# Rows scaled before they are turned, pair 1's keys ahead of a gate and its values ahead of pair 2's keys, and one inversion for head pairs 0 and 1

## The chip, the cores and the metric

The kernel runs on one core of a Trainium2 chip. A core has five engines with instruction streams of their own: TensorE (PE; its weight loads are listed as PEld), VectorE (DVE), ScalarE (ACT), GpSimd (POOL) and SyncE (SP), which issues nearly all the transfers here. The metric is the device time of one execution in microseconds; less is better.

## What is computed

One step of a decoder trunk of two layers, for a prompt of 1024 tokens and a sample group of 8 x 4 tokens, model width 1024, all in float32. Layer 0 is sliding-window attention, layer 1 a gated DeltaNet. Both have the form

```python
h = rms_norm(x, g) * (1 + scale[:, None]) + shift[:, None]   # shift, scale, gate = silu(c) @ w_mod + b_mod
x = x + gate * ((branch(h @ w_in) * silu(z)) @ w_out)
```

The DeltaNet has 8 key heads and 16 value heads of width 128 (two value heads to a key head), a causal convolution of four taps on q, k and v, and runs over chunks of tokens:

```python
lower = where(strict, (kb @ k.T) * decay, 0)                 # kb = k * beta
sol = triangular_solve(lower + I, rhs, lower=True, unit_diagonal=True)
u = w_v - w_k @ S                                            # w_v, w_k are the columns of sol
o = q_dec @ S + (q @ k.T * decay) @ u
S = S * g_tot + k_dec.T @ u
```

The last three lines are a chain: each chunk needs the state S of the one before.

## The kernel before, in words

**Projections.** The 1056 tokens are held transposed (model width on the partitions), in three groups of 384, 384 and 288. A projection takes 128 columns of a weight matrix; the float32 product is made of three products of split halves (high x high, high x low, low x high), so 128 columns cost 8 x 3 x 3 = 72 matmuls into the PSUM tiles `ps_pj`. ScalarE splits off the weights' high half (`wh`), GpSimd forms the low half (`wl`).

**Start (lines 600 to 740).** SyncE loads the nine tiles of x, `xt`, 128 tokens of 1024 each and 32 of the sample, then the modulation weights `wm` in two halves, the second into the buffers of the x rows as these come free. `scale_x` (627) takes the rows' norm `rs` and builds a diagonal `dg = ident * rs` of 128x128; `turn_x` (642) multiplies xt by it in float32, which scales and transposes at once: eight 128x128 blocks a tile, four to a PSUM bank, a "half tile" below. VectorE or ScalarE copies the result to `zo`. Then come the modulation steps (L344), their end (350 to 375), `shape_h` (662), which makes the split `hhi`, `hlo`, and the first projections (L702).

**The planner.** From the first attention projection on every instruction is issued through the class `Core` (96), which is why the profile gives all of them line 89. It keeps an estimated clock for each engine and for each tile. Work beside the projections is written as generators, "jobs", that yield a condition; `weave` (485) puts a job in a list by its rank (the tables `K` and `KR`), and after the projection matmuls `stages` lets each job whose condition holds issue its next piece. `ready` and `soon` are conditions on the planned TensorE clock, `idle` on another engine's, `later(n)` is a count of projection steps, and `until` lets jobs run, without projections, till a condition holds. So the order of each engine's instructions is fixed when the kernel is built, and it follows from the conditions, the ranks and the order in which the projections are called.

**End of layer 0.** The output projection takes its PSUM tiles by turns (1448), `add_out` (1336) adds the gated result to the rows, `shape` (1375) norms a tile with a diagonal as above, two packs of four blocks each, and makes `h2hi`, `h2lo`, the input of layer 1, tile by tile in the order 0, 8, 1, 2, 3, then the rest.

**Layer 1.** The 16 value heads go as eight pairs, r = 0 to 7, each with one key head. The loop at 2155 orders the projections; with q, k for the pair's query and key, z, z' for its gates and v, v' for its values it is: k0, q0, z0, z1, k1, v0, v0', q1, z2, z3, k2, v1, v1', q2 and so on, where a z pair is named by its place among the gates. `plan` (1631) is the same order for the weights' loads. Two lines hold a projection back:

```python
if what == "k":
    until(lambda: finished[0] >= r - 1)
```

so the keys of pair r + 1 wait until the chain of pair r - 1 is through. Beside these run, for each pair:
- the taps of the convolution (`vT<-XR,cT,vT` on VectorE),
- `solve` (1832), which builds the triangular blocks of 128 tokens for 8 blocks and 2 heads in `UZ`, and sends the sixty-four 32x32 diagonal blocks to DRAM,
- `invert` (1882), which loads these as `X`, one block to a partition (64 partitions), clears the blocks in UZ by 16 memsets on GpSimd, and inverts them by forward substitution on VectorE: 31 steps of two instructions (`tmp<-X`, then `X<-X,tmp`). The result goes to DRAM (`Xdd`) and comes back as `Xc`; `diagonal` makes `Xd` of it and multiplies it with UZ (`ps_lg<-Xd,UZ`), `blocks` forms the rest of the inverse (`ps_lg<-UZ,M`),
- `chain` (1984), the walk over the eight chunks with the state S. One chunk is `ps_mi<-S,kT`, `ps_ob<-vo,UZ`, `ps_mi<-us,ktok`, `ps_mi<-S,qT`, `ps_mi<-uo,DP` on TensorE with VectorE's `vo`, `us`, `uo` between.

`finished` counts chains, `inverted` and `solved` the pairs that are through these stages.

Of the kernel before, what the change touches and what calls it, by code (L numbers as in the profile page):

```python
# [219 lines left out]
def body(tc, I, O, cst_ap, dbg=None):  # L220
# [26 lines left out]
    VK = ()  # L247
# [379 lines left out]
    def scale_x(ts):  # L627

        n = len(ts)
        sv = sm.tile([P, 4], F32, tag="sv4", name="sv4")[:, 0:n]  # L630
        nc.vector.tensor_scalar(sv, xss[:, ts[0]:ts[0] + n], 1.0 / D, EPS, ALU.mult, ALU.add)
        rs = sm.tile([P, 4], F32, tag="rs4", name="rs4")[:, 0:n]
        rsqrt(nc, sm, rs, sv, n, tag=f"rx{n}")
        dgs = []
        for q, t in enumerate(ts):
            parts = P if t < NB else TS
            dg = xp.tile([P, P], F32, tag="dg", name="dg", bufs=6)[0:parts, 0:parts]
            last = nc.vector.tensor_scalar_mul(dg, ident[0:parts, 0:parts], rs[0:parts, q:q + 1])
            dgs.append(dg)
        return dgs, last  # L640

    def turn_x(ts, dgs, after):

        for q, t in enumerate(ts):
            parts = P if t < NB else TS
            for kk in range(2):
                pt = psb(("pj3", "lg", "pj3", "lg", "pj3", "ob")[(2 * t + kk) % 6])
                for j in range(4):
                    k = kk * 4 + j
                    mm = nc.tensor.matmul(pt[:, j * parts:(j + 1) * parts], xts[t][:, k * P:(k + 1) * P], dgs[q],  # L650
                                          start=True, stop=True)
# [56 lines left out]
    for i, ts in enumerate(xb):  # L708
        dgs, last = nxt
        if i < 3:  # L710
            nxt = scale_x(xb[i + 1])
        mm = turn_x(ts, dgs, nxt[1])
# [598 lines left out]
    if True:  # L1311
# [24 lines left out]
        def add_out(pj, i, t, hf):  # L1336
# [3 lines left out]
            yield lambda: gathered[0] == 2 * i + hf and i in rows_ and shaped[0] >= i - 1 + hf  # L1340
# [34 lines left out]
        def shape(i, t, xt, ss, parts):  # L1375

            nonlocal x2_guard
# [6 lines left out]
            dg = x2.tile([P, 512], F32, tag="y", name="dg", bufs=2)[0:parts, 0:parts]  # L1384
            nc.vector.tensor_scalar_mul(dg, ident[0:parts, 0:parts], rs)
            for kk in range(2):
                yield ready(dg, xt)
                pt = yield from bank("lg")
                for q in range(4):
                    nc.tensor.matmul(pt[:, q * parts:(q + 1) * parts], xt[:, (4 * kk + q) * P:(4 * kk + q + 1) * P], dg,  # L1390
                                     start=True, stop=True)
# [44 lines left out]
        for i, t in enumerate(turned_):  # L1436
# [7 lines left out]
            for kk, hf in order if i < NB else sorted(order, key=lambda o: o[::-1]):  # L1444
                if True:
                    ns = slice(hf * 512, (hf + 1) * 512)
                    if hf not in pjs:
                        tag = ("pj", "pj", "mi", "mi")[outs[0] % 4]
# [52 lines left out]
    def decays():  # L1501
# [21 lines left out]
        nc.scalar.activation(al, al, AF.Exp)  # L1523
        for gi, (a, b) in enumerate(GRP):
# [109 lines left out]
    for r in range(HQ):  # L1634
        pz, pv = [4096 + 2 * r * P, 4096 + (2 * r + 1) * P], [2 * HQ * P + 2 * r * P, 2 * HQ * P + (2 * r + 1) * P]
        pk = [(HQ + r + 1) * P]
        plan += [r * P] + (pz + (pv + pk if r in VK else pk + pv) if r + 1 < HQ else pv + pz)
# [5 lines left out]
    if True:  # L1643
# [188 lines left out]
        def solve(hq, st):  # L1832
# [47 lines left out]
            weave(invert(hq, st, Ld, Xdd), "invert", hq)  # L1880

        def invert(hq, st, Ld, Xdd):
            UZ, lg = st["UZ"], spare(hq)
            yield lambda: inverted[0] == hq


            X = gs.tile([64, 32, 32], F32, tag="X", name="X")
            tmp = gs.tile([64, 256], F32, tag="tmp", name="tmp")
            nc.sync.dma_start(X, Ld)
            yield soon(X)  # L1890
            nc.gpsimd.memset(X.rearrange("p i c -> p (i c)")[:, 0:1024:33], 1.0)
            for cp_ in range(4):
                uv = UZ[cp_].rearrange("p h c i -> p (h c) i")
                for b in range(4):
                    bs = slice(32 * b, 32 * b + 32)
                    nc.gpsimd.memset(uv[bs, :, bs], 0.0)
            yield soon(X)
            for k in range(31):
# [3 lines left out]
                nc.vector.tensor_tensor(tv, X[:, k, k + 1:].unsqueeze(2).to_broadcast([64, n, m]),  # L1902
                                        X[:, k, 0:m].unsqueeze(1).to_broadcast([64, n, m]), ALU.mult)
                nc.vector.tensor_tensor(X[:, k + 1:, 0:m], X[:, k + 1:, 0:m], tv, ALU.subtract)
            nc.sync.dma_start(Xdd, X)
            inverted[0] += 1
# [7 lines left out]
            def diagonal():  # L1914

                for cp_, uz in enumerate(uzs):
# [12 lines left out]
                    yield soon(pm)  # L1929
                    M = gs.tile([P, 4, 96], F32, tag="M", name="M", bufs=3)  # L1930
# [226 lines left out]
        for r in range(HQ):  # L2157
# [5 lines left out]
            if r + 1 < HQ:  # L2163
                proj_z(2 * r)
                proj_z(2 * r + 1)
# [3 lines left out]
                for what in "vk" if r in VK else "kv":  # L2169
                    if what == "k":  # L2170
# [546 lines left out]
```

## Time and profile before

| | us |
|---|---|
| median of three runs (1730.36 to 1739.1) | 1732.38 |
| the profiled execution's own time | 1730.22 |
| its span | 1728.1 |
| TensorE busy in it | 1628.6 |
| VectorE busy | 1207.9 |
| ScalarE busy | 862.0 |
| GpSimd busy | 603.2 |

The mean granted clock of TensorE is 0.983 of full speed. In a row of a timeline stand the start and the duration in us, the engine, the line, the operation and `out<-in` by the program's names, the shape, `x` and the count of matmuls that follow each other directly, and in brackets the idle time before with what ended it. A float32 matmul of the old `dg` kind has two records. Group rows end with the busy sum and the mean in ns of one, then the idle time just before them. Matmuls are pipelined, so the distance from one start to the next tells more of their cost than the duration.

### The profile page before, as it was taken

What the parts mean: (1) busy time and instruction counts of PE and PEld (TensorE: products, weight loads), DVE (VectorE), ACT (ScalarE), POOL (GpSimd) and SP (SyncE); (2) the same over time, 40 slices, a digit from 0 to 9 for tenths busy, and PEclk for the clock granted to TensorE, in tenths of its full rate; (3) what the DMA queues carried; (4) which work ended last, traced back from release to release, by engine and by line L of the source; (5) the groups of instructions that cost most, each with busy time, mean ns of one, the idle gap of its engine ahead of it and who ended that gap; (6) DMA issues with size and microseconds to landing.
All of it is one profiled execution on the core that took longest, in us unless ns stands there. A gap on an engine that the chain in (4) does not pass through costs nothing. (4 is left out here: it accounts for less than half of the span.)

```text
span 1728.1 us, 31800 instructions
## 1 busy us (share of the span) xinstructions
PE 1628.6 (94%) x10666; PEld 1432.1 (83%) x10666; DVE 1207.9 (70%) x3538; ACT 862.0 (50%) x2514; POOL 603.2 (35%) x1170
## 2 busy tenths in 40 slices
PE   6999999998999899799999999999999998989897
PEld 5988888986777889689989999899998996667685
DVE  4526675564565678877887789778798876357677
ACT  4625555444334565256554665654756555332332
POOL 2601111112122334354443544545345454332322
PEclk9999999999999999899999999999999999999999
DMA  9542121233233232132412323224232137764785
GB/s 330 152 134 72 52 58 50 55 98 106 85 130 103 81 79 67 53 88 56 126 36 75 102 59 107 69 77 112 50 107 62 46 97 211 228 200 130 233 277 184
DMA packets 281573, 191.77 MB, mean 111 GB/s; under 512 B 98362, under 2 KB 253882, under 8 KB 281379
## 3 DMA queue, kind: packets, MB, share of 16 engines
q1 hardware_dynamic: 281410, 189.75, 38.1%
q8 instruction: 84, 1.38, 0.3%
q14 instruction: 79, 0.64, 0.1%
HBM read 144.68 MB, written 47.04 MB: 111 GB/s over the span
## 5 line engine op out<-in xcount | busy, mean ns | idle before, releaser
L89 PE MATMUL ps_pj<-h2hi,wl 128*128 128x384 f32 (+1 forms) x1128 | 380.4, 337 | 2.2 <-POOL wl L89 2.2
L89 PE MATMUL ps_pj<-h2hi,wh 128*128 128x384 f32 (+1 forms) x1128 | 378.3, 335 | 2.1 <-ACT wh L89 2.1
L89 PE MATMUL ps_pj<-h2lo,wh 128*128 128x384 f32 (+1 forms) x1128 | 379.4, 336 | 0.0
L89 POOL TENSOR_TENSOR wl<-wr,wh 128x512 fp32r<-128x512 f32 x122 | 164.4, 1348 | 517.5 <-ACT wh L89 432.9
L89 PEld LDWEIGHTS ps_pj<-h2hi,wl 128*128 128x128 f32 x1128 | 213.6, 189 | 6.2 <-POOL wl L89 3.1
L89 PEld LDWEIGHTS ps_pj<-h2hi,wh 128*128 128x128 f32 x1128 | 213.5, 189 | 4.3 <-ACT wh L89 2.4
L89 PEld LDWEIGHTS ps_pj<-h2lo,wh 128*128 128x128 f32 x1128 | 213.5, 189 | 3.2
L89 POOL TENSOR_TENSOR xt<-xt,y 128x512 f32<-128x512 f32 (+1 forms) x48 | 63.9, 1333 | 188.2 <-DVE y L89 165.1
L89 PE MATMUL ps_pj<-hlo,wh 128*128 128x384 f32 (+1 forms) x360 | 119.0, 331 | 0.0
L89 PE MATMUL ps_pj<-hhi,wh 128*128 128x384 f32 (+1 forms) x360 | 118.4, 329 | 0.0
L89 PE MATMUL ps_pj<-hhi,wl 128*128 128x384 f32 (+1 forms) x360 | 117.9, 328 | 0.0
L89 DVE SCALAR_TENSOR_TENSOR vT<-XR,cT,vT 128x384 f32<-128x384 f32 (+1 forms) x144 | 93.0, 658 | 29.0 <-ACT vT L89 27.1
L89 DVE TENSOR_TENSOR tmp<-X 64x31 f32<-64x31 f32 (+15 forms) x248 | 94.0, 379 | 10.4 <-POOL X L89 7.1
L89 DVE TENSOR_TENSOR X<-X,tmp 64x31 f32<-64x31 f32 (+15 forms) x248 | 94.6, 381 | 8.5
L89 ACT CAST wh<-wr 128x512 fp32r<-128x512 f32 x122 | 75.1, 616 | 16.4 <-PE ps_pj L89 12.0
L89 PEld LDWEIGHTS ps_pj<-hlo,wh 128*128 128x128 f32 x360 | 67.7, 188 | 11.2 <-issue 11.1
L89 ACT COPY XR<-ps_pj 128x384 f32<-128x384 f32 (+1 forms) x96 | 43.0, 448 | 55.9 <-PE ps_pj L89 55.7
L89 POOL TENSOR_TENSOR Xd<-Xc,cst 32x128 f32<-32x128 f32 x128 | 63.4, 495 | 21.2 <-DMA Xc<-Xdd 10.4
L89 PEld LDWEIGHTS ps_pj<-hhi,wh 128*128 128x128 f32 x360 | 67.7, 188 | 2.7 <-issue 2.7
L89 ACT ACTIVATE prob<-prob,nm 128x256 f32<-128x256 f32 (+1 forms) x128 | 62.2, 489 | 14.8 <-DVE nm L89 14.6
L89 PEld LDWEIGHTS ps_pj<-hhi,wl 128*128 128x128 f32 x360 | 67.7, 188 | 2.1 <-issue 2.1
L89 ACT ACTIVATE vo<-vo,fo 128x128 f32<-128x128 f32 x128 | 42.3, 392 | 54.0 <-POOL fo L89 54.0
(574 smaller groups left out, 4218.1 us busy)
## 6 DMA issues: line engine op xcount, KB each, us to landing
wr<-in_gdn_w_in SPq DMA_DIRECT2D x96, 256.0 KB
S<-in_state_gdn_s SPq DMA_DIRECT2D x40, 256.0 KB
xt<-in_x_prompt SPq DMA_DIRECT2D x16, 512.0 KB
wm<-in_w_mod SPq DMA_DIRECT2D x16, 512.0 KB
wr<-in_swa_w_in SPq DMA_DIRECT2D x64, 128.0 KB
wmod<-in_w_mod SPq DMA_DIRECT2D x32, 256.0 KB
wm<-in_w_mod SPq DMA_DIRECT2D x32, 256.0 KB
DP<-gcr SPq DMA_DIRECT2D x64, 128.0 KB
```

The source lines that it names most:

```text
L89: inst = fn(*args, **kwargs)
```

## The change

Five parts, cut to their core:

```diff
-    VK = ()
+    VK = (1,)
...
 def scale_x(ts):
-            dg = xp.tile([P, P], F32, tag="dg", name="dg", bufs=6)[0:parts, 0:parts]
-            last = nc.vector.tensor_scalar_mul(dg, ident[0:parts, 0:parts], rs[0:parts, q:q + 1])
+            if t in (5, 7, 8):
+                nc.scalar.activation(xts[t], xts[t], AF.Copy, scale=rs[0:parts, q:q + 1])
+            else:
+                last = nc.vector.tensor_scalar_mul(xts[t], xts[t], rs[0:parts, q:q + 1])
...
 def turn_x(ts, after):
-                    mm = nc.tensor.matmul(pt[:, j * parts:(j + 1) * parts], xts[t][:, k * P:(k + 1) * P], dgs[q],
-                                          start=True, stop=True)
+                    mm = nc.tensor.transpose(pt[:, j * parts:(j + 1) * parts], xts[t][:, k * P:(k + 1) * P],
+                                             ident[0:parts, 0:parts])
...
 def add_out(pj, i, t, hf):
-            yield lambda: gathered[0] == 2 * i + hf and i in rows_ and shaped[0] >= i - 1 + hf
+            yield lambda: gathered[0] == 2 * i + hf and i in rows_
...
 def shape(i, t, xt, ss, parts):
+                if i < 5:
+                    xn = x2.tile([P, 512], F32, tag="xn", name="xn", bufs=2)[0:parts]
+                    yield idle("vector", rs, xt)
+                    nc.vector.tensor_scalar_mul(xn, xt[:, kk * 512:(kk + 1) * 512], rs)
...
+                    if i < 5:
+                        nc.tensor.transpose(pt[:, q * parts:(q + 1) * parts], xn[:, q * P:(q + 1) * P],
+                                            ident[0:parts, 0:parts])
...
-                        tag = ("pj", "pj", "mi", "mi")[outs[0] % 4]
+                        tag = ("mi", "mi", "pj", "pj")[outs[0] % 4]
...
 def decays():
+        yield later(KD)
         for gi, (a, b) in enumerate(GRP):
...
-        plan += [r * P] + (pz + (pv + pk if r in VK else pk + pv) if r + 1 < HQ else pv + pz)
+        plan += [r * P] + (pz[0:1] + pk + pz[1:] + pv if r == 0 else
+                           pz + (pv + pk if r in VK else pk + pv) if r + 1 < HQ else pv + pz)
...
-            weave(invert(hq, st, Ld, Xdd), "invert", hq)
+            blocks_of.append((hq, st, Ld, Xdd))
+            if hq != 0:
+                weave(invert(list(blocks_of)), "invert", hq)
+                blocks_of.clear()
...
 def invert(systems):
+            first, N = systems[0][0], 64 * len(systems)
+            X = gs.tile([P, 32, 32], F32, tag="X", name="X")[0:N]
+            for i, (_, _, Ld, _) in enumerate(systems):
+                nc.sync.dma_start(X[64 * i:64 * i + 64], Ld)
-            for cp_ in range(4):
-                uv = UZ[cp_].rearrange("p h c i -> p (h c) i")
-                for b in range(4):
-                    bs = slice(32 * b, 32 * b + 32)
-                    nc.gpsimd.memset(uv[bs, :, bs], 0.0)
...
+            for hq, st, _, Xdd in systems:
+                weave(rebuild(hq, st, Xdd), "invert", hq)
...
-                proj_z(2 * r + 1)
+                if r > 0:
+                    proj_z(2 * r + 1)
                 for what in "vk" if r in VK else "kv":
+                    if r == 0 and what == "v":
+                        proj_z(1)
```

- **Start.** The rows are scaled in place, six tiles on VectorE and three (5, 7, 8) on ScalarE, and then turned by transposes against the identity.
- **Shaping.** The first five tiles of `shape` are scaled half a row at a time into `xn` and turned the same way; the other four keep the diagonal. `add_out` no longer waits for `shaped`, and the output projection starts its turns with the other PSUM pair. `decays` starts eight projection steps later.
- **Order.** The projections run k0, q0, z0, k1, z1, v0, v0', q1, z2, z3, v1, v1', k2, q2: k1 and z1 change places, and the values of pair 1 go ahead of k2, whose condition is unchanged.
- **Joint inversion.** Pair 0's blocks wait until pair 1's are built; both are inverted together on 128 partitions. The other pairs are inverted alone, on 64. What came after the inversion in `invert` is now `rebuild`.
- **Memsets.** The 16 clearings of UZ in each pair are gone.

In TensorE's stream at the end of layer 0's output projection, where the projections of layer 1 begin (k0, its weights `kw0h` and `kw0l`), a pack with the diagonal `dg` stood behind the first three of them:

```order
L89 MATMUL ps_pj<-whi,olo 128x512
L89 MATMUL ps_pj<-wlo,ohi 128x512
L89 MATMUL ps_pj<-h2hi,kw0h 128x384
L89 MATMUL ps_pj<-h2lo,kw0h 128x384
L89 MATMUL ps_pj<-h2hi,kw0l 128x384
L89 MATMUL ps_lg<-dg,xt 128x128 x4
L89 MATMUL ps_pj<-h2hi,kw0h 128x384
```

Now that pack stands ahead of them, and the last one comes later, among the steps of the second half (`kw1h`, `kw1l`):

```order
L89 MATMUL ps_pj<-h2hi,kw0l 128x384
L89 MATMUL ps_pj<-h2hi,kw1h 128x384
L89 MATMUL ps_pj<-h2lo,kw1h 128x384
L89 MATMUL ps_pj<-h2hi,kw1l 128x384
L89 MATMUL ps_lg<-dg,xt 128x128 x4
L89 MATMUL ps_pj<-h2hi,kw1h 128x384
```

Between the first projection matmul and this pack there are 39 of them.

In TensorE's stream in the middle of chain 0, two chunks before read:

```order
L89 MATMUL ps_ob<-vo,UZ 128x128 x2
L89 MATMUL ps_mi<-us,ktok 128x256
L89 MATMUL ps_mi<-S,qT 128x256
L89 MATMUL ps_mi<-uo,DP 128x128 x2
L89 MATMUL ps_mi<-S,kT 128x256
L89 MATMUL ps_ob<-vo,UZ 128x128 x2
L89 MATMUL ps_tr<-cst,vo 128x128 x4
L89 MATMUL ps_mi<-us,ktok 128x256
L89 MATMUL ps_mi<-S,qT 128x256
L89 MATMUL ps_mi<-uo,DP 128x128 x2
```

Now one of its chunks is spread among the projection of v1:

```order
L89 MATMUL ps_pj<-h2lo,wh 128x384
L89 MATMUL ps_tr<-cst,vT 128x128 x2
L89 MATMUL ps_mi<-us,ktok 128x256
L89 MATMUL ps_lg<-Xd_6482,UZ 128x96 x4
L89 MATMUL ps_pj<-h2hi,wl 128x384
L89 MATMUL ps_mi<-S,qT 128x256
L89 MATMUL ps_mi<-uo,DP 128x128 x2
L89 MATMUL ps_pj<-h2hi,wh 128x384
L89 MATMUL ps_mi<-S,kT 128x256
L89 MATMUL ps_pj<-h2lo,wh 128x384
```

Five of the eight chunks stand like this; the last three still follow one another without a projection. In VectorE's stream the 62 instructions on X read `128x31` and so on for the two pairs where they read `64x31`, and stand behind the taps of v0':

```order
L89 SCALAR_TENSOR_TENSOR vT<-XR_6021,cT,vT 128x384 x6
L89 TENSOR_TENSOR tmp<-X 128x31
L89 TENSOR_TENSOR X<-X,tmp 128x31
L89 TENSOR_TENSOR tmp<-X 128x60
L89 TENSOR_TENSOR X<-X,tmp 128x30x2
```

45 lines of the change are left out of this document (24 added, 21 removed).

## The prediction

> **What bounds the kernel now.** I read the page first, for which engine is full; then the busy time by stage, for where that engine stands or works at something else; then the timeline of those places. The page (engines as busy us, share, instructions; then TensorE's granted clock in 40 slices):
>
> ```profile
> span 1728.1 us, 31800 instructions
> PE 1628.6 (94%) x10666; PEld 1432.1 (83%) x10666; DVE 1207.9 (70%) x3538; ACT 862.0 (50%) x2514; POOL 603.2 (35%) x1170
> PEclk9999999999999999899999999999999999999999
> ```
>
> TensorE is busy 94% of the span, so a gain has to come from the 99.5 us it stands, or from work that it needn't do or does with pauses that still count as busy. The second kind shows only by stage (stretch, its length, then busy us and count of PE, PEld, DVE, ACT, POOL, the granted clock, the DMA share and GB/s):
>
> ```profile
> 16.00:19.30 3.30, 3.30 (x16) 3.30 (x17) 2.08 (x11) 1.71 (x5) 0.00 (x0) 0.53 1.05 364
> 23.20:34.20 11.00, 10.96 (x96) 10.86 (x96) 7.27 (x24) 3.68 (x8) 0.00 (x0) 1.00 1.07 346
> 440.00:536.00 96.00, 96.00 (x480) 75.56 (x479) 56.67 (x176) 35.91 (x83) 20.71 (x16) 1.00 0.35 113
> 536.00:658.00 122.00, 109.16 (x691) 103.27 (x690) 82.67 (x231) 69.68 (x183) 40.43 (x72) 0.99 0.29 78
> 703.30:754.10 50.80, 38.21 (x280) 29.30 (x281) 41.80 (x126) 17.50 (x63) 15.71 (x54) 0.90 0.20 57
> 754.10:814.00 59.90, 59.55 (x417) 57.00 (x416) 45.93 (x115) 39.56 (x115) 25.76 (x61) 1.00 0.27 69
> ```
>
> Where projections are woven with the rest, TensorE is full: 59.55 of 59.90 us from 754. In 703 to 754 it shows 38.21 of 50.80, and the same stretch for the projections' bank alone shows none of them:
>
> ```profile
> 703.30:754.10 50.80, 0.00 (x0) 0.02 (x1) 0.00 (x0) 0.41 (x1) 0.90 0.20 57
> ```
>
> Its timeline has the last projection matmul, the walk of chain 0 with pauses, and the first of the next projection (start, us, engine, line, operation, in brackets the idle time before):
>
> ```profile
> 702.99 0.29 PE L89 MATMUL ps_pj<-h2hi,wl 128*128 128x288 f32 x1
> ...
> 733.13 0.75 PE L89 MATMUL ps_ob<-vo,UZ 128*128 128x128 f32 x4 [0.44 <-DVE vo L89]
> 734.59 0.70 PE L89 MATMUL ps_mi<-us,ktok 128*128 128x256 f32 x2 [0.70 <-DVE us L89]
> ...
> 737.40 0.74 PE L89 MATMUL ps_ob<-vo,UZ 128*128 128x128 f32 x4 [0.44 <-DVE vo L89]
> ...
> 754.11 0.42 PE L89 MATMUL ps_pj<-h2hi,wh 128*128 128x384 f32 x1
> ```
>
> This is the gate `finished[0] >= r - 1` of k2: after ten projections nothing but chain 0 and the blocks of pair 1 is left to TensorE. One chunk takes 4.27 us there (733.13 to 737.40), each step waiting for VectorE's result.
>
> **The start.** Today 12 half tiles are turned by f32 matmuls in 23.2 to 34.2, 0.89 us each by these rows; transposes of four 128x128 tiles take 0.36 (820.98 to 821.34):
>
> ```profile
> 28.67 1.06 PE L650 MATMUL ps_pj<-dg,xt 128*128 128x128 f32 x8
> 29.56 1.06 PE L650 MATMUL ps_lg<-dg,xt 128*128 128x128 f32 x8
> ...
> 34.23 3.64 PE L344 MATMUL ps_mi<-wm,cT 128*32 128x512 f32 x32
> ...
> 820.98 0.60 PE L89 MATMUL ps_lg<-cst,qT 128*128 128x128 f32 x4
> 821.34 0.42 PE L89 MATMUL ps_pj<-h2hi,wl 128*128 128x384 f32 x1
> ```
>
> On TensorE alone that is 12 x 0.53 = 6.4 us. The scaled rows add work elsewhere; the nearest rows are VectorE's whole-row scale, the diagonal it replaces, and ScalarE's pass over a row:
>
> ```profile
> L671 DVE TENSOR_SCALAR fu<-zo,Sc,Sh 128x1024 f32<-128x1024 f32 x2 | 1.6, 802 | 0.0
> L638 DVE TENSOR_SCALAR dg<-cst,rs 128x128 f32<-128x128 f32 x8 | 1.9, 283 | 0.1
> L625 ACT ACTIVATE sq<-xt 128x1024 f32<-128x1024 f32 x8 | 8.4, 1055 | 1.1 <-DMA xt<-in_x_prompt 1.0
> ```
>
> VectorE gets about three rows more in that stretch, less five diagonals: 7.27 + 2.4 - 1.4 = 8.3 us; ScalarE two rows more, 3.68 + 2.1 = 5.8. So VectorE's evacuations are late next, and the stretch shrinks from 11.0 to no less than about 8.3: -2.7. Beyond that, the modulation steps (3.64 us at 34.23) now stand partly among the transposes, in TensorE's new pauses: up to -3.6 more. And SyncE's queue, with the second half's weights on it, waits for exactly these matmuls to let the rows' buffers go:
>
> ```profile
> SPq L287 <- PE ps_lg L650: 10.1, 5, 4.7
> ```
>
> That is released sooner, but the DMA share is 1.07 already, so it can't bring much. I take -5, from -2 to -7.
>
> The granted clock was 0.53 in the first 3.3 us and 1.00 in the dense stretch; 0.90 where TensorE stood for a quarter (703 to 754). The Trainium skill, "TensorE: Matmul & The Clock Gate", Part 4 on PE-mode transpose, says that a transpose doesn't count as busy for the gate that raises the clock. No row here shows transposes alone, so nothing agrees or disagrees yet; by that rule the start is the second rival below.
>
> **The shaping.** Tiles 0, 8, 1, 2, 3 are turned the same way. The old packs and the only wait in front of one:
>
> ```profile
> L89 PE MATMUL ps_lg<-dg,xt 128*128 128x128 f32 x120 | 16.2, 278 | 2.0 <-DVE dg L89 2.0
> L89 PE MATMUL ps_lg<-dg,xt 32*128 32x32 f32 x16 | 2.1, 274 | 0.0
> 538.97 1.16 PE L89 MATMUL ps_lg<-dg,xt 128*128 128x128 f32 x8 [1.71 <-DVE dg L89]
> 539.88 0.42 PE L89 MATMUL ps_pj<-h2hi,kw0h 128*128 128x384 f32 x1
> ```
>
> A pack costs 0.91 (538.97 to 539.88), so eight save 8 x 0.55 = 4.4, and the sample tile's 2.1 falls to about 0.7. They lie in 440 to 536, where PE is busy 96.00 of 96.00: -5.8 at most. Ten half-row scales on VectorE (about 0.4 each, half of the 802) less five diagonals add 2.6 us to its 56.67 of 96; they are hidden unless a pack waits for its scale as the one above waited 1.71. I take -4.5, from 0 to -5.8. The dropped condition of `add_out` and the swapped banks of the output projection let the last rows be added earlier; the order now has 39 projection matmuls ahead of the last pack instead of three, so the 1.71 goes: -1.5, from 0 to -2. `decays` waiting for `later(KD)` moves small matmuls behind projections: 0.
>
> **The order of pairs 0 and 1.** Keys of pair 1 come before its gate, and v1, v1' before k2. Counted in completed projections, the changed order has chain 0's chunks behind 10.6, 10.9, 11.2, 11.4, 11.6 and then three times 12.0: five lie among v1's and v1' projections, three are bare. Bare: 3 x 4.27 = 12.8 us. The five cost TensorE only their work. Woven packs succeed one another like this:
>
> ```profile
> 823.62 0.59 PE L89 MATMUL ps_mi<-S,kT 128*128 128x256 f32 x2
> 824.05 0.59 PE L89 MATMUL ps_mi<-S,qT 128*128 128x256 f32 x2
> 824.48 0.61 PE L89 MATMUL ps_mi<-uo,DP 128*128 128x128 f32 x4
> 824.84 0.42 PE L89 MATMUL ps_pj<-h2lo,wh 128*128 128x384 f32 x1
> ```
>
> From start to start that is 0.43, 0.43, 0.36. With three packs on the state, two of four small ones and a transposed one (0.36 above) a chunk is 3 x 0.43 + 3 x 0.36 = 2.4 us, five are 12; the blocks of pair 1, an estimated eight packs of about a microsecond, bring it to 20. So the 50.8 become 12.8 + 20 = 33, a gain of 18, if the inversion is in time.
>
> **The joint inversion.** 62 instructions run once on 128 partitions instead of twice on 64, after the taps of v0'. That is the seventh projection, which ends at 658 in the old clock (the row from 536 above covers these seven); with an estimated 7 us for its taps the inversion starts at 665. The old ones (page, mean ns after the busy sum; then single instructions, last the first block that needs the result):
>
> ```profile
> L89 DVE TENSOR_TENSOR tmp<-X 64x31 f32<-64x31 f32 (+15 forms) x248 | 94.0, 379 | 10.4 <-POOL X L89 7.1
> L89 DVE TENSOR_TENSOR X<-X,tmp 64x31 f32<-64x31 f32 (+15 forms) x248 | 94.6, 381 | 8.5
> 630.91 1.30 DVE L89 TENSOR_TENSOR X<-X,tmp 64x112 f32<-64x112 f32 x1
> 681.32 0.27 DVE L89 TENSOR_TENSOR X<-X,tmp 64x112 f32<-64x112 f32 x1
> 682.90 0.18 DVE L89 TENSOR_TENSOR X<-X,tmp 64x31 f32<-64x31 f32 x1
> ...
> 691.91 1.03 PE L89 MATMUL ps_lg<-Xd,UZ 128*128 128x96 f32 x8
> ```
>
> 62 x 0.38 = 23.6 us, about 31 with other work of VectorE between; from the last one to the first block 691.91 - 683.08 = 8.8. Ready: 665 + 31 + 8.8 = 705. TensorE comes to that block when ten projections are done, 703 in the old clock. No row has 128 partitions: if the partitions cost nothing the wait is 0 to 3 us, at the mean of 0.5 it is 10. I take 4, from 0 to 14. Saved on VectorE: 23.6 us, off the path; so is GpSimd's, 128 memsets of 25.2 us:
>
> ```profile
> L89 POOL MEMSET UZ<- 32x128 f32 x128 | 25.2, 197 | 5.4
> ```
>
> This part: -18 + 4 = -14, from -4 to -20. From 14 projections on the two orders run together; the last chain starts 0.17 of a projection later, at 15 us each (754 to 814 is four of them), less what slack takes: +1, from -2 to +3.
>
> **The sum.** -5 - 4.5 - 1.5 - 14 + 1 = -24, from 1730.2 (the profiled execution's own time) to 1706.2. The median shown, 1732.4, is 2.2 above that execution: 1708.
>
> **Rivals.** First: chain 0 isn't covered. If the joint result comes 14 us or more after TensorE asks, or the chunks stall on VectorE as now, the bare stretch only moves: this part gives 0 to -4, the total is -10 to -14, 1718 to 1722. For: VectorE shows 41.80 of 50.80 busy there already, and chain 0 can't begin before both pairs are inverted. Against: 23.6 us less work on it. Chance 0.18.
>
> Second: the start at a low clock. If pauses between transposes keep the clock at the 0.53 of the first row, 12 x 0.36 us double (+4) and the modulation steps too (+3.6, part hidden by VectorE): that part gives -1 instead of -5, 1712. Chance 0.10.
>
> Third, slower: the joint instructions pay for their width, or for GpSimd beside them as the 1.30 against 0.27 above shows, at all 62. At 1.2 us each the result is ready at 665 + 74 + 8.8 = 748, and TensorE waits 45 us at the first block, with v1, v1' and k2 behind it: 45 instead of 4 makes +17, 1749. It turns slower past the bound when the wait exceeds 37 us, at 1.07 us an instruction. Against: one such row of 1.30 in a mean of 0.38. Chance 0.05. The Trainium skill, "SBUF — State Buffer", calls the port pair that VectorE and GpSimd share an exclusive lock, held for a whole instruction; the 1.30 and 0.27 agree.
>
> **The numbers.** Forecast 0.60; the three rivals 0.18, 0.10, 0.05; 0.07 for the small terms all at their poor ends (-2, 0, 0, with -13 and +1: 1718). A measurement tells 0.5% from no change, 8.7 us, so faster is below 1723.7: the forecast, the second rival and most of the first, 0.87; same 0.08; slower 0.05. The best ends together give -7 - 5.8 - 2 - 20 - 2 = -37, 1696; all poor ends without the third rival -3, 1729. Eight in ten: 1698 to 1723.
>
> **What would show it.** In the changed profile: projection matmuls between the chunks of chain 0 and about 13 us without any; the joint instructions near 0.38 us each and no idle above 5 us before the first block; half tiles turned in about 8 us from 23 and the first dense projection near 37; no wait on dg near 539. The forecast is wrong if the first block waits over 14 us, if chunks of chain 0 among projections still take 4 us of TensorE, or if the start ends where it did.

## The result and the profile after

| | before | after |
|---|---|---|
| median, us | 1734.36 (4 runs, 1730.36 to 1739.1) | 1712.32 (4 runs, 1711.98 to 1713.67) |
| the profiled execution | 1730.22 | 1712.31 |
| its span | 1728.1 | 1710.3 |

The ratio is 0.987, 95% interval 0.9845 to 0.9895: faster by 1.3%, clear of the noise, with 22 us between the medians and 17.9 between the profiled executions. A second measurement of the changed kernel gave 1712.54 and 0.9862 (0.9842 to 0.9882). The forecast was 1708, from 1698 to 1723. The profiled execution of the kernel before lies at the low end of its runs (1729.99 to 1741.15 over all of this record), so traces account for 17.9 us; where the rest lies, no trace shows.

The page of the changed kernel:

```profile
span 1710.3 us, 31377 instructions
PE 1613.3 (94%) x10554; PEld 1414.2 (83%) x10554; DVE 1189.9 (70%) x3478; ACT 864.7 (51%) x2517; POOL 578.4 (34%) x1041
```

TensorE's share is what it was. Its busy time fell by 15.3 us and its idle time by 2.5 (99.5 to 97.0): most of what went had counted as busy. The busy time by stage of the changed kernel comes next. The first row goes from the first projection of layer 1 (536.0 in the kernel before) to the end of seven (657.8 before); the others go from ten projections to the last projection matmul of the twelfth, from there to the first of the thirteenth (the stretch that is bare of projections), and on to the end of fourteen:

```profile
531.80:646.50 114.70, 107.74 (x685) 102.70 (x684) 75.80 (x212) 67.99 (x179) 32.19 (x55) 0.99 0.33 83
686.90:740.70 53.80, 53.41 (x486) 47.96 (x485) 35.88 (x88) 25.51 (x75) 25.82 (x57) 1.00 0.21 53
740.70:755.00 14.30, 10.45 (x54) 7.85 (x53) 7.88 (x25) 8.72 (x34) 8.52 (x32) 0.92 0.27 73
755.00:791.80 36.80, 36.14 (x231) 34.44 (x231) 28.09 (x82) 26.85 (x85) 13.47 (x36) 0.99 0.24 72
```

The stretch without projections shrank from 51 us to 14.3. The timeline of the changed kernel has the last projection matmul, the three chunks left over, and the next projection:

```profile
740.72 0.30 PE L89 MATMUL ps_pj<-h2hi,wl 128*128 128x288 f32 x1
740.85 0.61 PE L89 MATMUL ps_ob<-vo,UZ 128*128 128x128 f32 x4
...
745.75 0.61 PE L89 MATMUL ps_ob<-vo,UZ 128*128 128x128 f32 x4
...
751.08 0.75 PE L89 MATMUL ps_ob<-vo,UZ 128*128 128x128 f32 x4 [1.32 <-DVE vo L89]
...
755.04 0.67 PE L89 MATMUL ps_pj<-h2hi,wh 128*128 128x384 f32 x1
```

Counted by completed projections (one is done when the next begins), where both orders have done the same ones, the changed kernel is ahead by 3.4 us at its first dense projection (38.95 against 42.37), 4.2 at the first projection of layer 1, 11.4 after seven, 22.5 after fourteen, 24.3 at the last one, and 17.8 at the end. So 6.4 us are given back behind the last projection. The second measurement has a profile too. It is ahead by 4.6, 7.3, 14.5, 25.6, 26.1 and 17.7 at these places: a lead may differ by 3 us between two executions of one kernel.

### The profile page after: what moved, and what is told of

The parts are those of the page before. It is cut to its first block, busy times and chain, and to the rows that moved or that the text cites. A ratio compares the mean times of both kernels' runs of the same rounds, so it can differ in the third digit from the quotient of the medians.

```text
span 1710.3 us, 31377 instructions
## 1 busy us (share of the span) xinstructions
PE 1613.3 (94%) x10554; PEld 1414.2 (83%) x10554; DVE 1189.9 (70%) x3478; ACT 864.7 (51%) x2517; POOL 578.4 (34%) x1041
## 4 chain that ended last, share of the span: by engine, by line
PE 31%; DVE 8%; DMA 4%; ACT 3%; issue 2%; POOL 2%; SPq 1%; POOLq 0%; ACTq 0%; DVEq 0%
PE ps_pj L89 19%; PE ps_lg L89 4%; PE ps_mi L89 4%; PE ps_tr L89 3%; PE ps_ob L89 2%; DMA S<-in_state_gdn_s 1%; DMA of<-gTd 1%; DMA out_new_s_s<-S 1%; SPq L89 1%; DVE vT L89 1%; DVE tmp L89 1%; DVE UZ L89 1%; POOL rst L89 1%; DVE X L89 1%; ACT L89 0%
## 5 line engine op out<-in xcount | busy, mean ns | idle before, releaser
L89 DVE TENSOR_TENSOR tmp<-X 64x60 f32<-64x60 f32 (+23 forms) x217 | 82.3, 379 | 8.8 <-POOL X L89 5.4
L89 DVE TENSOR_TENSOR X<-X,tmp 64x60 f32<-64x60 f32 (+23 forms) x217 | 81.1, 374 | 7.5
L89 PEld LDWEIGHTS ps_pj<-hlo,wh 128*128 128x128 f32 x360 | 67.7, 188 | 11.2 <-issue 11.1
```

The costliest lines, as they stand in the source:

```text
L89: inst = fn(*args, **kwargs)
```

## The experiments

Each is the changed kernel with one edit. Times are medians; a ratio is to the kernel before on the same chip, with its 95% interval. The theory: the gain is chain 0 put among projections, with the forecast's 9.5 us (5 and 4.5) ahead of it from cheaper turning. The main rival: one part, or the joint inversion's spared VectorE work alone, does it.

### Inversions apart

```diff
-            if hq != 0:
+            if True:
                 weave(invert(list(blocks_of)), "invert", hq)
```

> The changed kernel with the blocks of pairs 0 and 1 inverted apart, 64 partitions each; all else stays. In its order all eight chunks of chain 0 stand behind the twelfth projection, none among v1 and v1'. Theory: the joint inversion is what lets chain 0 run among v1 and v1'; without it the stretch without projections grows from 14.3 to 35 to 50 us, and the whole is 18 to 30 us over the changed kernel (1730 to 1742). Rival: the joint inversion only spares VectorE work off the path; then within 3 us of the changed kernel.

1735.14, ratio 1.0003 (0.9988 to 1.0018): the whole gain is gone. The projections' bank in its bare stretch:

```profile
724.50:770.40 45.90, 0.34 (x3) 0.11 (x1) 0.00 (x0) 0.40 (x1) 1.00 0.22 55
```

The stretch is 45.9 us long again, only behind twelve projections instead of ten. Apart, pair 0 is inverted at 635.9 to 671.8 and pair 1 at 679.3 to 713.6, so pair 0's result is there early. But in the order that the planner makes, pair 0's first block stands behind 9.5 projections, the next behind 11.8, and all of chain 0 behind v1'. So what the joint inversion brings here is another order, not an earlier result (in the changed kernel it is there at 680.6); why the planner puts the blocks so late wasn't tried.

### Values of pair 1 behind the keys of pair 2

```diff
-    VK = (1,)
+    VK = ()
```

> The changed kernel with the values of pair 1 behind the keys of pair 2 again; keys of pair 1 ahead of the gate, the joint inversion and the rest stay. Theory: all eight chunks stand without projections behind the tenth one; the stretch without projections is 50 to 60 us instead of 14.3, of which some 20 were done among v1 and v1', so 15 to 25 us over the changed kernel, less up to 4 at the end, where chain 7 starts at 47.3 projections instead of 47.9: 1724 to 1735. Rival: the stretch was filled by the joint inversion alone, values or not; then within 3 us of the changed kernel.

1736.62, ratio 1.0004 (0.999 to 1.0019): also the whole gain. Its busy time while no projection runs:

```profile
686.30:743.90 57.60, 47.24 (x377) 35.64 (x377) 34.76 (x96) 18.73 (x65) 22.22 (x69) 0.88 0.17 49
```

57.6 us, longer than the 51 of before: the blocks of both pairs, which the joint inversion releases together, stand in it (256 of their matmuls, where 160 stood before). Without either of the two parts the time is that of the kernel before, so their gains can't be added up. The stretch alone doesn't explain the whole of it, as the table in the next section shows.

### The gate z1 ahead of the keys of pair 1

```diff
-        plan += [r * P] + (pz[0:1] + pk + pz[1:] + pv if r == 0 else
-                           pz + (pv + pk if r in VK else pk + pv) if r + 1 < HQ else pv + pz)
+        plan += [r * P] + (pz + (pv + pk if r in VK else pk + pv) if r + 1 < HQ else pv + pz)
...
-                if r > 0:
-                    proj_z(2 * r + 1)
+                proj_z(2 * r + 1)
...
-                    if r == 0 and what == "v":
-                        proj_z(1)
```

> The changed kernel with the gate z1 ahead of the keys of pair 1 again; the values of pair 1 ahead of the keys of pair 2, the joint inversion and the rest stay. In its order two of the eight chunks of chain 0 stand among v1 and v1', six behind them, and the first block of the joint inversion stands at 11.1 projections instead of 10.0. Theory: what counts is how many chunks stand without projections; six at 4.3 us and some blocks make a stretch of 26 to 32 us instead of 14.3, so 8 to 14 us over the changed kernel, less up to 2 at the end: 1719 to 1726. Rival: values ahead and the joint inversion do all, the keys nothing; then within 2 us of the changed kernel.

1722.33, ratio 0.9918 (0.9901 to 0.9934): 10 us over the changed kernel, within the 8 to 14 expected; the bare stretch is a little longer than expected:

```profile
722.00:756.20 34.20, 29.26 (x243) 22.95 (x241) 26.49 (x77) 18.73 (x70) 16.99 (x60) 1.00 0.24 65
```

34.2 us instead of 14.3. With three chunks bare, six, or eight the stretch has 14, 34 and 46 us, and 51 or 58 with eight in other orders. The time of the projections around it follows by a third to a half of that only: TensorE is busy in most of the stretch, with work that has to be done anyway. From the profiles, in us:

| | bare stretch | projections 8 to 14 | the last two projections | behind the last |
|---|---|---|---|---|
| kernel before | 51.1 | 156.5 | 36.3 | 284.8 |
| changed, two profiles | 14.3, 14.4 | 145.3, 145.4 | 34.2, 34.1 | 291.2, 293.1 |
| inversions apart | 45.9 | 161.1 | 39.6 | 289.2 |
| values behind | 57.7 | 159.6 | 45.8 | 288.2 |
| gate ahead | 34.2 | 153.4 | 40.6 | 287.6 |

In projections 8 to 14, where the theory puts the effect, these three edits cost 15.8, 14.3 and 8.1 us. The next largest part of their loss is at the other end of the program, in the last two projections, where two of the expectations had looked for a small gain.

### One more projection ahead of the keys of pair 2

```diff
+                    if r == 1 and what == "k":
+                        for j in (4, 5)[0:1]:
+                            proj_z(j)
                     if what == "k":
                         until(lambda: finished[0] >= r - 1)
```

The plan has z4 there, and pair 2 no longer calls it.

> The changed kernel with one projection more ahead of the keys of pair 2: the gate z4 of pair 2, which now comes behind v1'. In its order all eight chunks of chain 0 stand among projections (the last behind 12.5), and chain 7 starts behind 47.3 projections instead of 47.9. Theory: the last 14.3 us without projections, in which TensorE is busy 10.5 and has about 7 us of work to do, go; 6 to 9 us less, and 2 to 3 less at the end: 1700 to 1706, ratio 0.980 to 0.983. Rival: chain 0 then sets the pace in another place (k2 and pair 1 behind it), so the wait only moves: 1710 to 1713.

1733.81, ratio 0.9984 (0.9969 to 0.9999). My theory failed; the rival had the mechanism but not the size. The bare stretch of chain 0 is gone, and fourteen projections are done at 769.6 instead of 791.8. But they aren't the same ones: k2 is the fourteenth here, behind z4, and the thirteenth in the changed kernel, where it was done at 768.4. So k2 comes no sooner. The first chunk of chain 2 stands at the same time, here ahead of the row of the changed kernel:

```profile
893.91 0.71 PE L89 MATMUL ps_ob<-vo,UZ 128*128 128x128 f32 x4 [0.34 <-DVE UZ L89]
```

```profile
893.97 0.71 PE L89 MATMUL ps_ob<-vo,UZ 128*128 128x128 f32 x4
```

and then TensorE runs dry behind it (stretches ahead of and in the new bare one, of the kernel with z4 ahead):

```profile
882.00:920.40 38.40, 38.06 (x320) 35.72 (x318) 32.33 (x94) 14.04 (x48) 9.50 (x18) 1.00 0.27 74
920.40:942.70 22.30, 14.74 (x69) 11.64 (x68) 19.76 (x69) 6.22 (x22) 2.37 (x12) 0.85 0.27 65
```

The lead of 22 us was a gate drawn ahead, not a pair done sooner; at the next condition on `finished` it is paid back as a bare stretch of 22.3. After 24 projections this kernel is 3.9 us behind the changed one, after 46 it is 8.1, and 6.3 more are lost from there to the end (below). Its profiled execution, 1726.40, is the fastest of its twelve; where the median execution loses 7 us more, no trace shows.

### The old start

The old `scale_x` and `turn_x`, as in the lines with a minus of the change.

> The changed kernel with the old start (diagonals and float32 matmuls). Theory: the changed start is worth the 3.4 us by which its first dense projection comes earlier (38.95 against 42.37), and nothing behind it takes that up: first dense projection at 42.4 again, the whole about 3.5 us over the changed kernel, ratio to the kernel before 0.989. Rival: a later wait that ends at its own time takes it up; then within 1 us of the changed kernel, ratio 0.987. Also read: the cost of one half tile at 10, 17 and 25 us; the theory on the low clock (transposes from 16.4 to 25 cost 0.86 a pack, then 0.44 to 0.53) says that the float32 matmuls go from 1.7 to 0.9 near 19.4, as in the kernel before.

1717.78, ratio 0.9891 (0.987 to 0.9912): 5.5 us over the changed kernel, more than the theory's 3.5, in intervals that overlap. The first dense projection is back at 42.10 (3.15 later, or 4.4 against the second profile of the changed kernel); at the first projection of layer 1 it is 5.1 later, or 8.1, which is not explained. The theory on the pace was wrong about the moment: the float32 half tiles cost 0.99 at 15.7 us, 1.71 at 18.0, and about 0.9 from 23 on, instead of a single step near 19.4.

### Tiles 0 to 2 turned by the diagonal

```diff
+            if t < 3:
+                dgs[t] = xp.tile([P, P], F32, tag="dg", name="dg", bufs=3)
+                last = nc.vector.tensor_scalar_mul(dgs[t], ident, rs[:, q:q + 1])
+                continue
```

and `turn_x` takes the matmul with `dgs[t]` for these tiles.

> The changed kernel with tiles 0, 1 and 2 turned by the diagonal in float32 as before, the other six by transposes. Theory: the transposes from 16.4 to 25 us ran at half pace because they do not lift the clock, and matmuls there do; so the packs from 22.4 on cost 0.4 to 0.5 us from the first one instead of 0.86, and the first dense projection comes 1 to 2 us sooner (37 to 38 against 38.95): 1710.5 to 1711.5, a difference seen in the trace rather than in the time. Rival: the pace up to 25 us has nothing to do with the kind of matmul; then the packs at 22.4 to 25 cost 0.86 again and the first dense projection stays at 39 or later.

The start of the changed kernel (half tiles at their distance, then the first dense projection):

```profile
22.39 1.09 PE L650 MATMUL ps_pj<-cst,xt 128*128 128x128 f32 x4 [1.05 <-DVE xt L639]
23.26 1.06 PE L650 MATMUL ps_lg<-cst,xt 128*128 128x128 f32 x4
...
24.97 0.91 PE L650 MATMUL ps_lg<-cst,xt 128*128 128x128 f32 x4
25.72 0.60 PE L650 MATMUL ps_ob<-cst,xt 128*128 128x128 f32 x4
...
38.95 0.44 PE L702 MATMUL ps_pj<-hhi,wh 128*128 128x384 f32 x1
```

its stretch with the slow half tiles (the clock is the third number from the end),

```profile
22.30:24.90 2.60, 2.52 (x12) 2.55 (x13) 2.49 (x8) 2.31 (x5) 0.00 (x0) 1.00 1.04 385
```

and the start with the three tiles by matmul:

```profile
22.90 0.63 PE L660 MATMUL ps_pj<-cst,xt 128*128 128x128 f32 x4 [1.53 <-DVE xt L643]
23.36 0.60 PE L660 MATMUL ps_lg<-cst,xt 128*128 128x128 f32 x4
...
38.75 0.44 PE L712 MATMUL ps_pj<-hhi,wh 128*128 128x384 f32 x1
```

A half tile costs 0.46 instead of 0.87 from the first one, as the theory said, and yet the first dense projection is only 0.2 us earlier. But this doesn't show that matmuls lift the pace and transposes don't. In the second profile of the changed kernel, with nothing but transposes on TensorE since 9.85 us, the pace rises too, and earlier:

```profile
17.53 1.06 PE L650 MATMUL ps_tr<-cst,xt 128*128 128x128 f32 x4
18.38 0.79 PE L650 MATMUL ps_ob<-cst,xt 128*128 128x128 f32 x4
...
21.10 0.63 PE L650 MATMUL ps_pj<-cst,xt 128*128 128x128 f32 x4 [1.14 <-DVE xt L639]
21.56 0.60 PE L650 MATMUL ps_lg<-cst,xt 128*128 128x128 f32 x4
```

Eleven profiles of this record have all half tiles turned by transposes. In six the pace is doubled by 22 us, and the first dense projection stands at 37.7 to 38.3; in five it doubles about 25 us or later, and the projection stands at 38.8 to 40.0. So a slow half tile at 22 to 25 us goes with about 1 us, and what decides the moment stays open. With three tiles by matmul the projection stands at 38.75 in spite of the high pace; in this profile TensorE waits 1.53 us for the scaled rows ahead of 22.90. The whole was 1720.07, ratio 0.9907 (0.9884 to 0.9929), 6 to 8 us over the changed kernel; its profiled execution, the fastest of its six, shows 2.1 of them.

### All tiles of the shaping by the diagonal

```diff
-            if i >= 5:
-                dg = x2.tile([P, 512], F32, tag="xn", name="dg", bufs=2)[0:parts, 0:parts]
-                nc.vector.tensor_scalar_mul(dg, ident[0:parts, 0:parts], rs)
+            dg = x2.tile([P, 512], F32, tag="xn", name="dg", bufs=2)[0:parts, 0:parts]
+            nc.vector.tensor_scalar_mul(dg, ident[0:parts, 0:parts], rs)
```

and no `xn`.

> The changed kernel with all nine tiles of the shaping turned by a diagonal again. Theory: TensorE is full there, ten packs cost 0.4 to 0.55 us more each, so the first projections of layer 1 are about 4 to 5 us later and the whole is 4 us over the changed kernel, ratio 0.990. Rival: the packs wait for other things (rows, banks), and the whole stays within 1 us, ratio 0.987.

1718.83, ratio 0.9899 (0.988 to 0.9918); the first projection of layer 1 is 3.9 us later and the span 4.9 longer: the theory's 4 to 5, with ratios whose intervals overlap. The packs of the changed kernel,

```profile
L89 PE MATMUL ps_lg<-dg,xt 128*128 128x128 f32 x64 | 8.7, 278 | 1.3 <-issue 1.3
L89 PE MATMUL ps_lg<-cst,xn 128*128 128x128 f32 x32 | 4.9, 276 | 0.9 <-DVE xn L89 0.9
L89 PE MATMUL ps_lg<-cst,xn 32*128 32x32 f32 x8 | 0.9, 226 | 0.2 <-DVE xn L89 0.2
```

are 14.5 us busy where the experiment's are 17.3 + 2.1 = 19.4: 4.9 more, as much as the span is longer.

### `add_out`, the banks and `decays` as before

```diff
-            yield lambda: gathered[0] == 2 * i + hf and i in rows_
+            yield lambda: gathered[0] == 2 * i + hf and i in rows_ and shaped[0] >= i - 1 + hf
...
-                        tag = ("mi", "mi", "pj", "pj")[outs[0] % 4]
+                        tag = ("pj", "pj", "mi", "mi")[outs[0] % 4]
...
-        yield later(KD)
```

> The changed kernel with three small parts undone: add_out waits for the shaped tiles again, the output projection takes its banks in the old turn, and the small matmuls of decays come without the wait for eight steps. In its order the pack with the diagonal stands among the output projection and the matmuls of decays directly ahead of layer 1. Theory: these parts hide the wait of 1.7 us for dg and little else: 1 to 3 us over the changed kernel. Rival: they are the reason that the first seven projections of layer 1 take 114.7 us instead of 121.8; then 5 to 8 us over it.

1723.89, ratio 0.9933 (0.9915 to 0.995): 11 us over the changed kernel, more than either expected. The two longest waits are at the seam of the layers:

```profile
540.18 0.58 PE L89 MATMUL ps_lg<-h2hi,wab 128*64 128x384 f32 x1 [6.62 <-POOL wab L89]
...
563.84 2.04 PE L89 MATMUL ps_lg<-dg,xt 128*128 128x128 f32 x8 [3.62 <-DVE dg L89]
```

Without `later(KD)` the matmuls of `decays` stand ahead of the first projection, and TensorE waits 6.62 us for weights that GpSimd is still splitting. The kernel before had no such wait, though it lacked the line too: there these matmuls stand behind twenty projection matmuls, at 543.84. I had costed that line at 0. Since the three edits were undone together, the 11 us are those of all three; the wait of 6.62 is what the trace puts down to this line.

### The clearings of UZ back

```diff
             nc.gpsimd.memset(X.rearrange("p i c -> p (i c)")[:, 0:1024:33], 1.0)
+            for _, st_, _, _ in systems:
+                for cp_ in range(4):
+                    uv = st_["UZ"][cp_].rearrange("p h c i -> p (h c) i")
+                    for b in range(4):
+                        bs = slice(32 * b, 32 * b + 32)
+                        nc.gpsimd.memset(uv[bs, :, bs], 0.0)
```

> The changed kernel with GpSimd's 16 clearings of UZ in each pair back, issued ahead of the inversion. Theory: 25 us of GpSimd, which is busy for a third of the time, are off the path, and the inversion waits some 3 us more for each pair ahead of work that has slack: within 1.5 us of the changed kernel. Rival: the clearings of 32 instructions stand in front of the joint inversion, which has no slack; then the first block is 4 to 7 us later and the whole 4 to 7 us longer.

1727.96, ratio 0.9945 (0.9929 to 0.9961): 15 us over the changed kernel of the same chip, and neither story holds. The 32 clearings do have a price on TensorE that neither named, since they stand in GpSimd's queue ahead of the split of the weights (two rows of the timeline, then a stretch):

```profile
645.25 7.63 POOL L89 MEMSET UZ<- 32x128 f32 x32
654.28 0.69 PE L89 MATMUL ps_pj<-h2hi,wl 128*128 128x384 f32 x1 [2.28 <-POOL wl L89]
650.00:660.00 10.00, 6.50 (x24) 6.19 (x25) 9.48 (x20) 2.36 (x6) 8.06 (x22) 0.66 0.22 57
```

From 650 to 660 TensorE does 24 matmuls at a granted clock of 0.66, where the changed kernel does 59 at 1.00. But the order is another one here, with all eight chunks of chain 0 begun among projections and the bare stretch down to some 5 us, and by the fourteenth projection the two balance: 8 to 14 take 144.2 us instead of 145.3. The first block stands at 687.0 (changed: 687.8 and 684.7), fourteen projections are done at 790.5 (791.8 and 788.7), and forty at 1272.1 (1273.4 and 1271.6). So most of the loss is in the last two projections, here ahead of the same stretch of the changed kernel:

```profile
1388.10:1433.80 45.70, 40.89 (x322) 37.12 (x321) 24.91 (x71) 17.17 (x45) 20.29 (x42) 0.96 0.37 109
```

```profile
1384.80:1419.10 34.30, 33.97 (x279) 31.86 (x278) 23.83 (x60) 17.83 (x47) 23.48 (x43) 1.00 0.54 153
```

The clearings shift the planner's clock and the order comes out another: chain 7 starts behind 47.3 projections instead of 47.9, so 43 more matmuls, and waits, stand ahead of the last projection. From 46 projections to the end this kernel takes 336.5 us, the one with z4 ahead 331.7 and the one with values behind 334, all three with chain 7 at 47.3; two with chain 7 at 47.5 take 328 and 329, and the eight profiles with it at 47.9 take 321 to 329. But the kernel before, with 47.7, takes 321 as well. That the place of chain 7 is the cause is thus argued from these fourteen profiles, not shown by moving it alone.

### The selector's load earlier, and the changed kernel again

One kernel issues the load of `selt` ahead of that of `ong`, with this edit; the other ahead of the last weight loads too, with the first three lines earlier in the program:

```diff
+        o_, w_ = COFF["selp"]
+        selp = wp.tile([P, w_], F32, tag="wr", name="selt", bufs=4)
+        nc.sync.dma_start(selp, cst_ap[:, o_:o_ + w_])
-        weave(gate_rows(gate, "selp", lambda: gathered.__setitem__(0, 0)), "prepare")
+        weave(gate_rows(gate, "selp", lambda: gathered.__setitem__(0, 0), selp), "prepare")
```

> The changed kernel with the load of the last gate's selector (selt) issued ahead of the small load ong, whose issue took SyncE 3.23 us. Theory: the 6 us given back behind the last projection are partly this: in the changed kernel TensorE stood 2.65 us at 1430 for selt, and the output projection's rows behind it; the load lands about 3 us earlier, so the end comes 2 to 3 us earlier: 1709 to 1710. Rival: the pace of chain 7 and the rows of the output projection set the end; then within 0.7 us of the changed kernel.

> The changed kernel itself, to stand beside the others of this call on the same chip: ratio to the kernel before 0.985 to 0.990.

> The changed kernel with the load of the last gate's selector issued earlier still: ahead of three weight loads, of qk and of ong. Moved ahead of ong alone it left TensorE 1.71 us of wait instead of 2.65 and the ratio came to 0.984. Theory: the end is set by this load, so 2 to 5 us less than the changed kernel of this call. Rival: what was seen there was the scatter of the runs; then within 1 us of it.

What they were made for is the seam behind the last projection. SyncE's queue and TensorE in the changed kernel:

```profile
1424.64 3.23 SPq L89 DMA_DIRECT2D ong<-in_gdn_o_norm_g  x1
1427.97 0.38 SPq L89 DMA_DIRECT2D selt<-in_cst  x1
...
1430.13 3.78 PE L89 MATMUL ps_lg<-modG,selt 128*128 128x512 f32 x4 [2.65 <-DMA selt<-in_cst]
...
1434.42 0.77 PE L89 MATMUL ps_pj<-h2hi,ohi 128*128 128x512 f32 x1
```

The last row is the first matmul of the output projection, 15.3 us behind the last projection (1419.1). In the kernel before it came 6.9 us behind (1443.3), 4.65 after its rows `of` were asked for:

```profile
1445.59 0.43 SPq L89 DMA_DIRECT2D of<-gTd  x1
...
1450.24 0.49 PE L89 MATMUL ps_pj<-h2hi,ohi 128*128 128x512 f32 x1
```

With selt ahead of the weight loads:

```profile
1420.54 2.06 PE L89 MATMUL ps_lg<-modG,selt 128*128 128x512 f32 x4
...
1428.23 0.47 PE L89 MATMUL ps_pj<-h2hi,ohi 128*128 128x512 f32 x1 [3.13 <-issue]
```

The wait for selt is gone and the output projection starts 12.6 us behind the last projection instead of 15.3. With the smaller move it isn't the load of `ong` that takes long, but the one that now stands in its place:

```profile
1423.70 2.81 SPq L89 DMA_DIRECT2D selt<-in_cst  x1
1426.56 0.42 SPq L89 DMA_DIRECT2D ong<-in_gdn_o_norm_g  x1
```

So the 3.23 us belonged to the place in the queue and not to `ong`, to which the expectation gave them. The wait for selt is 1.71 there instead of 2.65, and the output projection starts 15.2 us behind the last projection, hardly sooner than in the changed kernel. The earlier move measured 1708.25, ratio 0.983 (0.9811 to 0.985), the smaller move 1708.28, ratio 0.9838 (0.9815 to 0.9861), and the changed kernel beside the former 1712.54, ratio 0.9862 (0.9842 to 0.9882). Both medians are 4 us better, in intervals that overlap: likely, not settled, and for the smaller move the trace shows nothing to account for it. The earlier move has the lowest median of this study, hardly below the smaller one.

## Why the prediction was right, step by step

The direction, the range and the main mechanism held: the gate at k2 left TensorE with chain 0 and the blocks, and five of the chunks went among projections. In the profiled executions, -24 was forecast and -17.9 measured. By the terms of the sum, for both profiles of the changed kernel:

| step | forecast | first profile | second profile |
|---|---|---|---|
| start | -5 | -3.4 | -4.6 |
| shaping and the wait for dg, to the second projection of layer 1 | -6 | -3.2 | -5.1 |
| up to seven projections | 0 | -4.7 | -4.8 |
| bare stretch, projections 8 to 14 | -14 | -11.1 | -11.1 |
| 14 to the last projection | 0 | -1.8 | -0.5 |
| behind the last projection | +1 | +6.4 | +8.4 |
| sum | -24 | -17.8 | -17.7 |

That the sum came so near is partly luck: some 5 to 6.5 us that I hadn't forecast, ahead of the stretch and behind it, made up for about half of what the other terms fell short.

- **The start** was mis-sized. I counted a pack at 0.36 from the first one, where packs at 16 to 25 us took about 0.87 in the first profile. That is the second rival's mechanism in part: the pace doubled at 25 us there, where it had doubled at 19.4 in the kernel before. The clock rows don't show it; they read 1.00 in this stretch, too, while the durations are twice the later ones. The Trainium skill, "TensorE: Matmul & The Clock Gate", Part 4 on PE-mode transpose, says that the full clock doesn't engage for transposes, which don't count as busy the same way. The traces disagree: in the second profile the pace rose at 18.4 us after transposes alone, and there the start gave 4.6 of the 5 us.
- **The shaping** held in size: the span is 4.9 us longer when it is undone. The wait for dg didn't go, it shrank from 1.71 to 1.13, with "issue" as its end.
- **Up to seven projections** was missed. The kernel before waited there in rows that I hadn't weighed:

```profile
600.52 0.44 PE L89 MATMUL ps_pj<-h2hi,wh 128*128 128x384 f32 x1 [2.11 <-ACT wh L89]
601.87 0.44 PE L89 MATMUL ps_pj<-h2hi,wl 128*128 128x384 f32 x1 [0.73 <-POOL wl L89]
642.67 0.55 PE L89 MATMUL ps_tr<-cst,vT 128*128 128x128 f32 x3 [3.69 <-ACT vT L89]
```

  These 6.5 us are gone; none of the changed kernel's waits from 580 to 646 is above 1.00. With the inversions apart the seven projections take 117.4 us instead of 114.7. There, as in the kernel before, VectorE begins to invert pair 0 among them, so a part of the gain is probably that it no longer does.
- **The bare stretch** came out at 14.3 us against 12.8 forecast, and the joint inversion as costed. That the term is -11 and not -14 has another reason. The 4 us of wait didn't come, but the chunks and blocks among projections cost more than the 20 us that I took: the four projections behind the tenth took 60.1 us beside the bare stretch before and 90.7 now, and only 4.9 of these 30.6 were taken out of the three projections ahead (45.3 to 40.4), where a part of pair 0's blocks had stood. I had left pair 0's blocks out. The groups of the inversions, the ends of the joint one, and the first block:

```profile
L89 DVE TENSOR_TENSOR tmp<-X 64x60 f32<-64x60 f32 (+23 forms) x217 | 82.3, 379 | 8.8 <-POOL X L89 5.4
L89 DVE TENSOR_TENSOR X<-X,tmp 64x60 f32<-64x60 f32 (+23 forms) x217 | 81.1, 374 | 7.5
647.51 0.18 DVE L89 TENSOR_TENSOR tmp<-X 128x31 f32<-128x31 f32 x1
680.45 0.19 DVE L89 TENSOR_TENSOR X<-X,tmp 128x31 f32<-128x31 f32 x1
...
687.77 0.46 PE L89 MATMUL ps_lg<-Xd,UZ 128*128 128x96 f32 x2 [0.39 <-POOL Xd L89]
```

  The joint 62 instructions are 23.2 us busy (forecast 23.6) in 33 us (forecast 31). They begin at 647.5, 1 us behind the seventh projection where I took 7 for the taps, and so the wait at the first block is 0.39 where I took 4. The third rival is out: 128 partitions cost what 64 do. The first rival is out as well, but the two runs at ratio 1.000 show how near it was: one part less and chain 0 is bare again.
- **Behind the last projection** is the step that failed most: +1 was forecast from chain 7's later start. It is the output projection's first matmul, 15.3 instead of 6.9 us behind the last projection, of which a shorter rest (275.9 for 277.9 us) gives 2 back: 6.4. The load of selt and what stands ahead of it in SyncE's queue is a part, 2.7 us of it with the earlier load; the rest is open.
- **The clearings, and `later(KD)` with the two small parts**, cost 15 and 11 us when undone, where the sum has nothing for the clearings and `later(KD)`. For the clearings most of it stands in the last two projections, far from the work that they are, and only the moved order was found there. In a planned order an edit's price is that of the order that comes out, and I had read the order only around the pairs 0 and 1.

## What to carry to other kernels

Find where the fullest engine does something other than its main work, and what gate holds the main work back; count what stands bare there before and after, and take off what has to be done anyway: here a stretch shorter by 37 us gave 11. In these runs filling the hole paid where the work drawn ahead brought the next gate nearer: values and keys did, a gate's projection did not. Where a planner sets the order, compare the whole order, its last seam too, for each part of a change alone, since parts that are worth 20 us together may be worth nothing apart. Take a second profile of the same kernel before a difference of 3 us between two traces is explained.

## What the runs showed of the hardware

- An instruction of VectorE on 128 partitions took as long as on 64: 62 of them 23.2 us joint, and 21.8 to 27.0 us alone in the kernel before.
- A pack of four float32 transposes took about 0.87 us at first and 0.44 to 0.46 later, while the clock read 1.00 in both stretches; the change came between 18 and 27 us, at another moment in each profile, and in four of the eleven after transposes alone. A pack of float32 matmuls with a diagonal took 0.9 at the high pace.
- In SyncE's queue near the end, the load that came right behind `qk` occupied it for 3.23 and 2.33 us (`ong`, two profiles) or 2.81 (`selt` in its place), and the next one for 0.38 to 0.42, whichever of the two it was.
